# Casts of the weights rank first among ready work when the engines' queues are laid out

## The chip, the core and the metric

The kernel runs on one core of one Trainium2 chip. The metric is the device time of one execution in microseconds (us); a kernel's time is the median over its runs. The core's engines are TensorE (PE, the matrix products), VectorE (DVE), ScalarE (ACT), GpSimd (POOL) and SyncE (SP, which issues DMAs here). Each works through a queue of its own, in the order in which the program was laid out.

## What is computed

Two blocks follow one another on 512 tokens of width 1024, all in float32. The first is a half step of SwiGLU, an attention stage of two branches (a native sparse one, NSA, and a sliding window with sinks, SWA), and another half step of SwiGLU. The second is an adaptive normalisation, a mixer (HGRN2 on one half of the width, S5 on the other), and a PEER layer: 8 heads pick experts by two products of keys, and the outputs of 16384 experts of one unit each are summed.

```python
h = h + 0.5 * swiglu(rmsnorm(h), ffn1_gate, ffn1_up, ffn1_down)
u = rmsnorm(h); q, k, v, ... = split(u @ w_in)
merged = sigmoid(ga) * (nsa(...) @ w_branch_a) + sigmoid(gb) * (swa(...) @ w_branch_b)
h = h + merged @ w_out
h = h + 0.5 * swiglu(rmsnorm(h), ffn2_gate, ffn2_up, ffn2_down)
x = rmsnorm(h)
...
x = x + gt1 * (concat(hgrn2(q, f, i, g), s5(u)) @ w_out)
x = x + gt2 * peer(h2, peer_wq, keys1, keys2, peer_u, peer_v)
return rmsnorm(x)
```

## The kernel before

Every product with a weight goes the same way. `Prog.weight` loads a tile of 128x1024 float32 (`raw`) by a DMA that SP issues, ACT copies it to fp32r, the format that the matmuls take (`whi`, L173), and DVE subtracts the two for the rest (`wlo`, L174; on POOL in a part of the first PEER stage, while `pool_lo` is set). The activations are split alike (`xhi`, `xlo`). `mm3` then makes three matmuls of one: `whi` by `xhi`, `whi` by `xlo`, `wlo` by `xhi`, all into one PSUM tile `ps`. The line of all matmuls is L82, that of the transposes L86. I call the two casts the hi cast and the lo cast.

The tiles `raw`, `whi` and `wlo` come from the pool `w` with three buffers each. So the hi cast of a weight writes over that of the third weight before it, and can't start until PE has read that one for the last time. `Weights.take` prepares a weight up to two ahead of its use (`AHEAD = 2`).

The order of the work is set twice. The program is written as generators, which `weave` lets take turns by an estimated clock; that gives every instruction its rank. Then the scheduler of the tile framework lays out the queue of each engine: among the instructions that are ready by its estimate, the one of the lowest rank number is put next. The result is fixed when the kernel is built. On the chip each engine takes its queue strictly from the front, and an instruction at the front that waits for a buffer or an operand holds up all that stand behind it.

The names and lines that come up below: in attention, `t` are the scores' exponentials (ACT, L923 in NSA and L966 in SWA), `sums` their sums, `fac` the reciprocal (DVE L927 and L973), by which DVE scales `t` (L934, L976). PE transposes `t` (L86), ACT and DVE copy the transposes out of PSUM (L656), and PE multiplies them with the values (`nat`). In the mixer, `hg_head` builds a head's decay in seven levels: PE multiplies, DVE takes the level over by a predicated copy (L1326) and makes the next operands (L1308, L1309). In the second PEER stage the activations come back from memory, POOL multiplies them with the gates, and ACT and DVE split them into `pwh` (L590) and `pwl` (L591).

Of the kernel before, what the change touches and what calls it, by code (L numbers as in the profile page):

```python
# [8 lines left out]
F32 = mybir.dt.float32  # L9
# [4 lines left out]
ALU = mybir.AluOpType  # L14
# [35 lines left out]
class Prog:  # L50
# [116 lines left out]
    def weight(self, ap, n=1024):  # L167
        nc = self.nc
        raw = self.w.tile([128, 1024], F32, tag="raw", name=self.name("raw"))
        nc.sync.dma_start(raw[:, :n], ap)  # L170
        hi = self.w.tile([128, 1024], F32R, tag="whi", name=self.name("whi"))
        lo = self.w.tile([128, 1024], F32R, tag="wlo", name=self.name("wlo"))
        nc.scalar.copy(hi[:, :n], raw[:, :n])  # L173
        (nc.gpsimd if self.pool_lo else nc.vector).tensor_tensor(lo[:, :n], raw[:, :n], hi[:, :n].bitcast(F32),  # L174
                                                                 op=ALU.subtract)
        return raw, hi, lo

    def mm3(self, ps, whi, wlo, xhi, xlo, start, stop):
# [1761 lines left out]
```

## Time and profile before

| what | value |
|---|---|
| median of 3 runs | 3066.33 us (3066.26 to 3071.9) |
| the profiled execution | 3077.48 us |
| its span, first to last instruction | 3075.7 us |
| mean granted TensorE clock | 0.992 of full speed |
| PE busy | 3007.1 us, 98% |
| DVE, ACT, POOL busy | 67%, 38%, 35% |

The profile is of one execution, which took 11.15 us more than the median; the rows' times are those of that execution. A row of the timeline gives the start, the duration, the engine, the line and operation, and, where the engine was idle before it, for how long and which instruction ended that. In the page's names `ps` is a PSUM tile and buffer numbers are left out. The stages lie about so in the span: first SwiGLU to 400 us, attention to 750, second SwiGLU and the preparation of S5 to 1185, mixer to 1475, first PEER stage (routing, then products with `peer_u` and the dense gates) to 2341, second PEER stage (products with `peer_v`) to 3062.

### The profile page before, as it was taken

Reading aid. Unit: us, or ns where it says so; the run is one execution under the profiler, and the core shown is the slowest. Engines: PE = TensorE matmul, PEld = TensorE weight load, DVE = VectorE, ACT = ScalarE, POOL = GpSimd, SP = SyncE. Lnnn points to the kernel's source line nnn. Section 1 sums busy time; section 2 is a strip of 40 time slices with the busy share of each in tenths; the row PEclk is TensorE's granted clock in tenths of the full one; section 3 lists DMA queues with packets and bytes.
Section 4 is the critical chain, followed back from the end, with each engine's and each line's share of the span. In section 5 each row is a group of like instructions: output and inputs, shape, how many; then the busy total and the mean of one; then the engine's idle time right before and its main releaser. Section 6 shows DMA issues by size and latency. Waiting matters only on the chain.

```text
span 3075.7 us, 39979 instructions
## 1 busy us (share of the span) xinstructions
PE 3007.1 (98%) x14672; PEld 2473.4 (80%) x14672; DVE 2058.7 (67%) x3797; ACT 1167.1 (38%) x1851; POOL 1091.0 (35%) x1025
## 2 busy tenths in 40 slices
PE   8999999999999999899999899999999999999998
PEld 7888876667887889787888778888887888888887
DVE  7455467775768656874778999878773656655653
ACT  4222334453422235443434344444443322332232
POOL 1000110002353422012345798878772423322321
PEclk9999999999999999999999999999999999999999
DMA  6344322113535443222333355555558656555642
GB/s 203 109 143 132 102 81 83 49 39 100 164 117 184 161 127 117 77 71 83 99 110 117 127 185 188 190 179 197 186 185 268 215 192 205 192 187 190 204 137 76
DMA packets 140323, 443.53 MB, mean 144 GB/s; under 512 B 16720, under 2 KB 19568, under 8 KB 135008
## 3 DMA queue, kind: packets, MB, share of 16 engines
q1 hardware_dynamic: 82512, 285.41, 28.9%
q10 hardware_dynamic: 42624, 101.73, 9.0%
q0 software_dynamic: 14992, 53.85, 5.5%
q8 instruction: 116, 1.90, 0.3%
q14 instruction: 79, 0.65, 0.1%
HBM read 361.88 MB, written 77.86 MB: 143 GB/s over the span
## 4 chain that ended last, share of the span: by engine, by line
PE 70%; DVE 6%; issue 1%; POOL 1%; DMA 1%; ACT 1%; ACTq 0%; DVEq 0%; POOLq 0%
PE ps L82 69%; DVE wlo L174 1%; PE ps L86 1%; DMA t<-act_d 1%; DVE b L1570 1%; POOL t L823 0%; POOL eq L1550 0%; DVE eq L1546 0%; ACT whi L173 0%; DMA act_d<-t 0%; DVE sel L1553 0%; POOL t L1687 0%; DVE stage L1595 0%; DVE h L1817 0%; ACT t L966 0%
## 5 line engine op out<-in xcount | busy, mean ns | idle before, releaser
L173 ACT CAST whi<-raw 128x1024 fp32r<-128x1024 f32 (+2 forms) x505 | 516.9, 1026 | 1113.9 <-PE ps L82 881.2
L82 PE MATMUL ps<-xhi,whi 128*128 128x512 f32 (+1 forms) x2232 | 875.2, 393 | 12.2 <-ACT whi L173 9.8
L82 PE MATMUL ps<-xhi,wlo 128*128 128x512 f32 (+1 forms) x2232 | 864.2, 388 | 9.6 <-DVE wlo L174 9.5
L82 PE MATMUL ps<-xlo,whi 128*128 128x512 f32 (+1 forms) x2232 | 864.2, 388 | 0.8 <-DVE xlo L382 0.7
L174 DVE TENSOR_TENSOR wlo<-raw,whi 128x1024 fp32r<-128x1024 f32 (+2 forms) x476 | 610.9, 1284 | 129.1 <-ACT whi L173 118.9
L82 PEld LDWEIGHTS ps<-xhi,whi 128*128 128x128 f32 x2232 | 421.8, 189 | 105.6 <-issue 14.1
L82 PEld LDWEIGHTS ps<-xhi,wlo 128*128 128x128 f32 x2232 | 421.3, 189 | 99.7 <-DVE wlo L174 12.4
L82 PEld LDWEIGHTS ps<-xlo,whi 128*128 128x128 f32 x2232 | 421.6, 189 | 80.8 <-issue 2.5
L1569 POOL TENSOR_SCALAR a<-iota,routeT 128x128 fp32r<-128x128 f32 x512 | 452.5, 900 | 95.6 <-PE ps L82 91.7
L82 PE MATMUL ps<-pwh,wlo 128*128 128x512 f32 (+1 forms) x1048 | 402.5, 384 | 2.1 <-DVE wlo L174 2.1
L82 PE MATMUL ps<-pwh,whi 128*128 128x512 f32 (+1 forms) x1048 | 402.9, 385 | 1.1 <-ACT pwh L590 1.1
L82 PE MATMUL ps<-pwl,whi 128*128 128x512 f32 (+1 forms) x1048 | 402.8, 384 | 0.2 <-DVE pwl L591 0.2
L1687 POOL TENSOR_TENSOR t<-t,gt 128x512 f32<-128x512 f32 x128 | 196.6, 1556 | 422.9 <-DMA t<-act_d 389.0
L1570 DVE SCALAR_TENSOR_TENSOR b<-iota,routeT,routeG 128x256 fp32r<-128x256 f32 x512 | 242.8, 523 | 63.7 <-PE ps L82 63.7
L1823 DVE SCALAR_TENSOR_TENSOR h<-ps,mod,h 128x512 f32<-128x512 f32 (+1 forms) x131 | 96.3, 735 | 218.4 <-PE ps L82 218.4
L82 PEld LDWEIGHTS ps<-pwh,wlo 128*128 128x128 f32 x1048 | 196.9, 188 | 41.4 <-DVE wlo L174 2.6
L82 PEld LDWEIGHTS ps<-pwh,whi 128*128 128x128 f32 x1048 | 196.9, 188 | 40.6 <-ACT pwh L590 1.8
L82 PEld LDWEIGHTS ps<-pwl,whi 128*128 128x128 f32 x1048 | 196.9, 188 | 39.9 <-DVE pwl L591 1.0
L1594 ACT COPY stage<-ps 128x256 f32<-128x256 f32 x256 | 137.8, 643 | 151.2 <-PE ps L82 142.3
L591 DVE TENSOR_TENSOR pwl<-t,pwh 128x512 fp32r<-128x512 f32 x128 | 141.0, 1128 | 46.7 <-ACT pwh L590 42.1
L268 POOL TENSOR_TENSOR acc<-acc,sq 128x512 f32<-128x512 f32 x18 | 32.0, 1777 | 382.4 <-ACT sq L264 382.0
L1595 DVE TENSOR_TENSOR stage<-stage,ps 128x256 f32<-128x256 f32 x256 | 146.8, 620 | 2.3 <-ACT stage L1594 2.3
(407 smaller groups left out, 3841.5 us busy)
## 6 DMA issues: line engine op xcount, KB each, us to landing
raw<-pu SPq DMA_DIRECT2D x128, 512.0 KB, 3.6
raw<-pv SPq DMA_DIRECT2D x128, 512.0 KB, 3.5
act_d<-t ACTq DMA_DIRECT2D x128, 256.0 KB, 2.8
gates_d<-stage ACTq DMA_DIRECT2D x32, 1024.0 KB, 4.2
gt<-gates_d POOLq DMA_DIRECT2D x16, 2048.0 KB, 13.6
t<-act_d ACTq DMA_DIRECT2D x128, 256.0 KB, 3.6
aw<-ada_w SPq DMA_DIRECT2D x48, 512.0 KB, 4.5
raw<-g SPq DMA_DIRECT2D x44, 512.0 KB, 3.6
```

The lines of the kernel that those rows point to most:

```text
L82: self.nc.tensor.matmul(out, lhsT=lhsT, rhs=rhs, start=start, stop=stop)
L86: self.nc.tensor.transpose(out, x, ident)
L173: nc.scalar.copy(hi[:, :n], raw[:, :n])
L174: (nc.gpsimd if self.pool_lo else nc.vector).tensor_tensor(lo[:, :n], raw[:, :n], hi[:, :n].bitcast(F32), op=ALU.subtract)
L268: nc.gpsimd.tensor_tensor(st["acc"], st["acc"], sq, op=ALU.add)
L591: self.nc.vector.tensor_tensor(lo, x, hi.bitcast(F32), op=ALU.subtract)
L1569: g.tensor_scalar(a[:, i, :], iota, T2[0][:, c], None, op0=ALU.is_equal)
L1570: v.scalar_tensor_tensor(b[:, i], iota[:, None, :].to_broadcast([128, 2, 128]), T2[1][:, c], TG[:, t + i, :, None].to_broadcast([128, 2, 1 ...
L1594: nc.scalar.copy(sv, pv[:, :, 0])
L1595: v.tensor_tensor(sv, sv, pv[:, :, 1], op=ALU.add)
L1687: g.tensor_tensor(f(t), f(t), gts[e // 8][:, :, e % 8, :], op=ALU.mult)
L1823: nc.vector.scalar_tensor_tensor(x, ps, P.mod[:, 40 + d:41 + d], x, op0=ALU.mult, op1=ALU.add)
```

## The change

The two casts in `Prog.weight` are put under `high_priority()`. This gives them the first rank among ready work when the queues are laid out, in place of the rank of their position in the program. No instruction is added, taken away or altered, and on the chip nothing is ranked: only places in the five queues differ.

```diff
-        nc.scalar.copy(hi[:, :n], raw[:, :n])
-        (nc.gpsimd if self.pool_lo else nc.vector).tensor_tensor(lo[:, :n], raw[:, :n], hi[:, :n].bitcast(F32),
-                                                                 op=ALU.subtract)
+
+        with self.tc.high_priority():
+            nc.scalar.copy(hi[:, :n], raw[:, :n])
+            (nc.gpsimd if self.pool_lo else nc.vector).tensor_tensor(lo[:, :n], raw[:, :n], hi[:, :n].bitcast(F32),
+                                                                     op=ALU.subtract)
```

The lines behind the edit move down by two. Of some 13,790 instructions that the queue of PE holds, 193 rows of a comparison differ, of 3,511 on DVE 332, of 2,021 on ACT 177, of 1,030 on POOL 13, on SP none. The lo casts `wlo_7295`, `wlo_7853`, `wlo_14230`, `wlo_14265`, `wlo_14309`, `wlo_14344` have the same neighbours in both orders, and so have all rows of PE from 1780 to 2341 us and all rows of all engines from 2400 us on. The number behind a name is that of the tile, in the order of the program.

The first place is at 650 us, in the last NSA block. ACT computes the exponentials of four score tiles in eight instructions, and the order there was:

```order
L923 ACTIVATE t_5137,sums_5121<-ps_5123,mx_5120 128x256 x2
L923 ACTIVATE t_5149,sums_5121<-ps_5140,mx_5120 128x256 x2
L923 ACTIVATE t_5155,sums_5121<-ps_5141,mx_5120 128x256 x2
L885 ACTIVATE cm_5183,sums_5197<-cm_5183,mx_5196 128x31 x8
L656 COPY t_5228<-ps_5218 128x512
L173 CAST whi_5238<-raw_5236 128x1024
```

It is now the following, on ACT:

```order
L925 ACTIVATE t_5137,sums_5121<-ps_5123,mx_5120 128x256 x2
L925 ACTIVATE t_5149,sums_5121<-ps_5140,mx_5120 128x256 x2
L925 ACTIVATE t_5155,sums_5121<-ps_5141,mx_5120 128x256
L175 CAST whi_5238<-raw_5236 128x1024
L925 ACTIVATE t_5155,sums_5121<-ps_5141,mx_5120 128x256
L887 ACTIVATE cm_5183,sums_5197<-cm_5183,mx_5196 128x31 x8
L658 COPY t_5228<-ps_5218 128x512
```

The hi cast of weight 5238 has gone ahead of the last exponential, of eight instructions on `cm` and of a copy. On DVE, at the same place, the reciprocal of the sums was followed by the scaling, and the lo cast came later:

```order
L927 RECIPROCAL fac_5158<-sums_5121 128x8
L931 TENSOR_TENSOR fac_5158<-fac_5158,gates 128x8
L934 TENSOR_SCALAR t_5131<-t_5131,fac_5158 128x256 x2
L934 TENSOR_SCALAR t_5149<-t_5149,fac_5158 128x256 x2
L934 TENSOR_SCALAR t_5137<-t_5137,fac_5158 128x256 x2
L934 TENSOR_SCALAR t_5155<-t_5155,fac_5158 128x256 x2
L888 RECIPROCAL fac_5208<-sums_5197 128x8
L889 TENSOR_TENSOR fac_5208<-fac_5208,gates 128x8
L656 COPY t_5230<-ps_5219 128x512
L892 TENSOR_TENSOR cm_5183<-cm_5183,fac_5208 128x248
L811 TENSOR_TENSOR t_5232<-ps_5091,rb_2797 128x512
L174 TENSOR_TENSOR wlo_5239<-raw_5236,whi_5238 128x1024
```

After the change the lo cast stands ahead of the reciprocal, on DVE:

```order
L885 TENSOR_SCALAR mx_5196<-mx_5196 128x8
L176 TENSOR_TENSOR wlo_5239<-raw_5236,whi_5238 128x1024
L929 RECIPROCAL fac_5158<-sums_5121 128x8
L933 TENSOR_TENSOR fac_5158<-fac_5158,gates 128x8
L936 TENSOR_SCALAR t_5131<-t_5131,fac_5158 128x256 x2
L936 TENSOR_SCALAR t_5149<-t_5149,fac_5158 128x256 x2
```

So the reciprocal and all scaling rows are now behind a cast that waits for the hi cast.

The second place is at 608 us, in SWA, on DVE. `t_4746` and `t_4782` are transposes that PE needs for the products with the values; before:

```order
L969 TENSOR_TENSOR es_4679<-mx_4677,sinks 128x8
L656 COPY t_4746<-ps_4735 128x512
L971 TENSOR_TENSOR sums_4678<-sums_4678,es_4679 128x8
L811 TENSOR_TENSOR t_4754<-ps_4646,rb_2797 128x512
L973 RECIPROCAL fac_4723<-sums_4678 128x8
L656 COPY t_4782<-ps_4771 128x512
L976 TENSOR_SCALAR t_4690<-t_4690,fac_4723 128x256 x2
L976 TENSOR_SCALAR t_4710<-t_4710,fac_4723 128x256 x2
L976 TENSOR_SCALAR t_4697<-t_4697,fac_4723 128x256 x2
L976 TENSOR_SCALAR t_4717<-t_4717,fac_4723 128x256 x2
L656 COPY t_2734<-ps_4733 128x128
L174 TENSOR_TENSOR wlo_4832<-raw_4829,whi_4831 128x1024
```

After the change, the same stretch of DVE reads:

```order
L971 TENSOR_TENSOR es_4679<-mx_4677,sinks 128x8
L176 TENSOR_TENSOR wlo_4832<-raw_4829,whi_4831 128x1024
L973 TENSOR_TENSOR sums_4678<-sums_4678,es_4679 128x8
L658 COPY t_4746<-ps_4735 128x512
L975 RECIPROCAL fac_4723<-sums_4678 128x8
L813 TENSOR_TENSOR t_4754<-ps_4646,rb_2797 128x512
L978 TENSOR_SCALAR t_4690<-t_4690,fac_4723 128x256 x2
L978 TENSOR_SCALAR t_4710<-t_4710,fac_4723 128x256 x2
L978 TENSOR_SCALAR t_4697<-t_4697,fac_4723 128x256 x2
L978 TENSOR_SCALAR t_4717<-t_4717,fac_4723 128x256 x2
L658 COPY t_4782<-ps_4771 128x512
```

The lo cast 4832 has moved from the row behind the scaling to the row ahead of `sums_4678`, and with it the copies `t_4746` and `t_4782` have moved back. On ACT the hi cast 4831 has moved ahead of `es_4679` and of the copy of `t_4744`. Of the same kind are `wlo_4761` and the copy `t_4635` (596 us), `wlo_3712` and the copy `t_3700` (494 us), and `wlo_5423` with the scaling of `t_5374` (675 us).

The third place is at 1258 us, the last levels of an HGRN2 head, on DVE. Before:

```order
L1018 TENSOR_TENSOR t_10082<-t_9793 128x4x64 x2
L1326 COPY_PREDICATED t_9842<-c_lvl,ps_10077 128x512
L174 TENSOR_TENSOR wlo_10098<-raw_10095,whi_10097 128x1024
L1308 TENSOR_TENSOR t_10082<-t_9792,t_10082 128x4x64
L1309 TENSOR_TENSOR t_10082<-t_9801,t_10082 128x4x64
L1326 COPY_PREDICATED t_9842<-c_lvl,ps_10113 128x512
```

After the change DVE goes through the same levels so:

```order
L1020 TENSOR_TENSOR t_10082<-t_9793 128x4x64 x2
L1328 COPY_PREDICATED t_9842<-c_lvl,ps_10077 128x512
L658 COPY t_10143<-ps_9804 128x8x16
L1310 TENSOR_TENSOR t_10082<-t_9792,t_10082 128x4x64
L1311 TENSOR_TENSOR t_10082<-t_9801,t_10082 128x4x64
L1328 COPY_PREDICATED t_9842<-c_lvl,ps_10113 128x512
```

The lo cast 10098 is gone from between them, since it and the lo casts 10020 and 10167 now stand 51, 63 and 35 rows ahead of the row L1310 here, among earlier levels; `wlo_10167` stood behind all levels before. A copy of `t_10143` has moved forward too. At the begin of the second PEER stage (2390 us) the move goes the other way: `wlo_20877`, which stood ahead of `pwl_20980` and `pwl_21019`, now stands behind both.

## Rows read from the trace of the kernel before

**Rows 1.** the page, busy time of each engine

```profile
PE 3007.1 (98%) x14672; PEld 2473.4 (80%) x14672; DVE 2058.7 (67%) x3797; ACT 1167.1 (38%) x1851; POOL 1091.0 (35%) x1025
```

**Rows 2.** the page's groups: count | busy, mean ns | idle before, releaser

```profile
L173 ACT CAST whi<-raw 128x1024 fp32r<-128x1024 f32 (+2 forms) x505 | 516.9, 1026 | 1113.9 <-PE ps L82 881.2
```

**Rows 3.** waits of PE: us in total, times, longest

```profile
PE ps L82 <- DVE wlo L174: 15.6, 9, 3.4
PE ps L82 <- ACT whi L173: 11.0, 3, 9.8
```

**Rows 4.** instructions of tile wlo, 1696 to 1728 us: who waited for it

```profile
  PE ps L82: 8.4, 4
```

**Rows 5.** windows, PE alone: busy (instructions), PEclk, DMA share, GB/s

```profile
1780.00:2340.00 560.00, 559.96 (x2678) 1.00 0.56 193
1709.00:1712.00 3.00, 3.00 (x7) 0.50 0.78 236
```

**Rows 6.** timeline at 2388 to 2399 us, begin of the second PEER stage

```profile
2387.77 1.23 DVE L174 TENSOR_TENSOR wlo<-raw,whi 128x1024 fp32r<-128x1024 f32 x1 [0.83 <-ACT whi L173]
...
2388.91 4.31 DVE L591 TENSOR_TENSOR pwl<-t,pwh 128x512 fp32r<-128x512 f32 x3
...
2394.70 4.42 DVE L174 TENSOR_TENSOR wlo<-raw,whi 128x1024 fp32r<-128x1024 f32 x1 [0.82 <-ACT whi L173]
...
2399.18 0.50 PE L82 MATMUL ps<-pwh,wlo 128*128 128x512 f32 x1 [2.14 <-DVE wlo L174]
```

**Rows 7.** timeline at 650 us: start, us, engine, line, [idle before <-releaser]

```profile
650.75 0.48 ACT L923 ACTIVATE t<-ps,mx 128x256 f32<-128x256 f32 x1
...
651.35 0.20 DVE L927 RECIPROCAL fac<-sums 128x8 f32<-128x8 f32 x1 [0.86 <-ACT t L923]
...
652.28 1.35 PE L86 MATMUL ps<-ident,t 128*128 128x128 f32 x5 [1.45 <-DVE t L934]
...
654.09 1.06 ACT L173 CAST whi<-raw 128x1024 fp32r<-128x1024 f32 x1
```

**Rows 8.** timeline at 1260 us, a head of HGRN2

```profile
1260.28 0.72 DVE L1326 COPY_PREDICATED t<-c_lvl,ps 128x512 f32<-128x512 int32 x1
...
1260.50 2.04 PE L82 MATMUL ps<-t 128*128 128x128 f32 x8 [2.92 <-DVE t L1309]
...
1264.00 1.21 DVE L174 TENSOR_TENSOR wlo<-raw,whi 128x1024 fp32r<-128x1024 f32 x1
```

**Rows 9.** timeline at 607 to 610 us

```profile
607.83 0.68 DVE L656 COPY t<-ps 128x512 f32<-128x512 f32 x1
...
609.45 0.23 ACT L970 ACTIVATE es<-es 128x8 f32<-128x8 f32 x1
...
610.02 1.09 ACT L173 CAST whi<-raw 128x1024 fp32r<-128x1024 f32 x1
...
610.21 1.08 PE L82 MATMUL ps<-t,nat 128*64 128x512 f32 x4 [0.66 <-ACT t L656]
```

**Rows 10.** timeline at two more places in the attention stage

```profile
493.66 0.41 DVE L656 COPY t<-ps 128x256 f32<-128x256 f32 x1
...
495.15 0.65 PE L82 MATMUL ps<-t,nat 128*64 128x256 f32 x4 [0.49 <-ACT t L656]
...
595.97 0.68 DVE L656 COPY t<-ps 128x512 f32<-128x512 f32 x1
...
597.53 1.08 PE L82 MATMUL ps<-t,nat 128*64 128x512 f32 x4 [0.48 <-ACT t L656]
```

**Rows 11.** windows: us, busy (instructions) of PE, PEld, DVE, ACT, POOL, PEclk

```profile
911.53:922.50 10.97, 9.89 (x44) 7.86 (x42) 10.97 (x3) 1.68 (x2) 10.94 (x11) 1.00 0.07 25
1224.00:1261.00 37.00, 28.35 (x161) 27.02 (x161) 36.43 (x85) 13.72 (x21) 0.00 (x0) 0.92 0.10 31
```

**Rows 12.** timeline, two single rows of DVE and PE

```profile
911.53 10.97 DVE L174 TENSOR_TENSOR wlo<-raw,whi 128x1024 fp32r<-128x1024 f32 x1
...
1708.89 0.79 PE L82 MATMUL ps<-xhi,wlo 128*128 128x512 f32 x1 [3.43 <-DVE wlo L174]
```

## The prediction

> **What bounds the kernel now.** I read the busy times first: PE is busy 3007.1 of the span's 3075.7 us [rows 1], so what a change can win is bounded by the other 69 us, and what it loses is whatever new wait it puts on PE. Then the group of the hi casts: in front of them ACT is idle 1113.9 us, and 881.2 of these end with a matmul of PE [rows 2]. Most casts, then, wait for the buffer of the third weight before them, which PE still reads. A cast that waits for a buffer gains nothing from a better place in its queue.
>
> Then the waits of PE. Over the whole execution PE waits 15.6 us, nine times, for a lo cast, and 11.0 us, three times, for a hi cast, of which 9.8 us are one wait, the first weight at the program's start [rows 3]. So the casts that the change promotes cost PE at most 15.6 + 11.0 - 9.8 = 16.8 us. Of the 15.6 us, 8.4 lie in four waits at the end of PEER's routing, 1696 to 1728 us [rows 4]. Last I looked at the dense stage, 1780 to 2340 us: PE is busy 559.96 of 560.00 us [rows 5], no wait is left there to take away.
>
> **What the change takes away.** The four casts behind the 8.4 us (14230, 14265, 14309, 14344) and the one with the slow row below (7295) keep their neighbours in the new order. They were already at the place where the scheduler thought their buffer free; on the chip DVE is simply full there. What the promotion can reach is less than the other 16.8 - 8.4 = 8.4 us, and one wait of that, 2.14 us at 2399 us [rows 6], belongs to a stage where a neighbouring cast moves back. I take 0 for the gain, with up to 2 us as the better end: the waits for hi casts other than the first sum to 1.2 us [rows 3], and in the NSA compression, where those casts do move forward, PE then finds the lo cast late in their place.
>
> **What it adds, place by place.** Every term is a cast that now stands ahead of a row that PE waits for. The durations are 1.06 us for the hi cast [rows 7] and 1.21 for the lo cast [rows 8].
>
> At 650 us PE waits 1.45 us for the scaled exponentials already [rows 7]. The last exponential starts at 650.75 us. In the new order the hi cast 5238 runs first, 650.75 to 651.81, and the last exponential with its sum ends near 652.4 instead of 651.3. DVE has the lo cast at its front, starts it when the hi cast is done, at about 651.85, and ends near 653.06. Only then comes the reciprocal, which ran at 651.35: 1.7 us late, and the transposes of PE behind it as much. PE's rows ahead of them are unchanged, so nothing covers it: +1.7, wait 3.2 in all.
>
> At 608 us PE waits 0.66 us for ACT's copy of a transpose [rows 9]. ACT would start the hi cast 4831 at 609.45 in place of 610.02, so that the copy is about 1.1 late. The other copy that PE's row at 610.21 needs, `t_4746`, ran at 607.83 [rows 9]; it now stands behind the lo cast (about 610.55 to 611.75) and the sums, and ends near 612.5, 2.3 us after PE wants it. PE gets some of that back, since one of the four products is moved behind its next weight and a later wait for the same kind of copy closes. Between 1.1 and 2.3 I take +1.6.
>
> Three more places in attention have this pattern. At 596 us the copy `t_4635` moves from 595.97 to behind the lo cast, and PE wants it at 597.53 [rows 10]; it would end near 599.85, but PE's next rows waited for the scaling anyway, which ends only about 0.9 later: +0.9. At 494 us the copy `t_3700` moves from 493.66 to behind both casts, near 496.8, and PE's product of 495.15 [rows 10] needs it; about 0.65 us of other matmuls move ahead to cover it: +1.0. At 675 us the scaling of `t_5374` goes behind both casts, 1.5 us late, with some 0.4 us of slack: +1.1. Together +3.0, the ends being 0.9 (matmuls pulled forward cover the rest) and 2.3 + 1.6 + 1.5 = 5.4 (nothing is covered).
>
> In the HGRN2 head PE waits 2.92 us until 1260.50 for DVE [rows 8], which is full from 1224 to 1261 us, with 36.43 of 37.00 us busy [rows 11]. Three lo casts move further ahead on DVE, which changes nothing for the last level as long as they were ahead of it. The fourth, 10167, ran at 1264.00, behind the levels [rows 8], and now runs ahead of them, with one small copy: 1.21 + 0.14 = +1.4 in front of the last level. The ends are 0 (a matmul group pulled forward on PE covers it) and 2.4 (DVE also waits for the hi cast's buffer once more).
>
> At the begin of the second PEER stage the lo cast 20877 moves from 2387.77 to behind two of the three `pwl` rows that ran from 2388.91 to 2393.22 [rows 6] and a row of `h`. It would end near 2394.4. PE wanted the lo cast after it at 2399.18 - 2.14 = 2397.0 [rows 6], and goes through the 24 matmuls of a weight in 24 x 560/2678 = 5.0 us [rows 5], so it wants 20877 near 2392.0: a new wait of 2.4 us. The wait of 2.14 us, for a cast that took 4.42 us [rows 6], is then swallowed, at least in part. Between -2.1 and +2.4 I take +0.5.
>
> The rest (one or two rows moved at 630 us, at the begin of the mixer, and at its end) is below 0.3 us a place: +0.3 in all, 0 to 1.5. In the dense stage some thirty hi casts go ahead of one gelu and its DMA, and lo casts ahead of one or two additions; PE's order is the same and PE has no wait there [rows 5], so 0.
>
> A longer wait costs once more when the clock falls. After the wait of 3.43 us that ended at 1708.89 [rows 12] PE ran 3.0 us at a granted clock of 0.50, that is at 1.2 GHz [rows 5]: half of them, 1.5 us, are lost. The wait at 650 us would grow to this length. I take +1.0, between 0 and 3.
>
> **A rule on this.** The lo cast at 911.53 us took 10.97 us [rows 12], nine times a usual one, while POOL was busy through the stretch [rows 11]. The Trainium skill, page "SBUF — State Buffer", section "SBUF: two separate sides", says that VectorE and GpSimd share a pair of ports under an exclusive lock, and that the loser is blocked until the other's instruction is done. By that rule one POOL instruction is the most that a cast waits, and a cast moved next to POOL's work would cost some 10.94/11 = 1.0 us [rows 11]; by the row it is up to 10.97 - 1.21 = 9.8, over most of the eleven instructions that POOL ran there. The sum is the same by either, since no cast of the terms above stands beside POOL's runs except 20877.
>
> **The sum.** 1.7 + 1.6 + 3.0 + 1.4 + 0.5 + 0.3 + 1.0 = +9.5 us. The profiled execution would come to 3077.5 + 9.5 = 3087.0, and the median, which lies 11.2 below it, to 3075.8. The lower ends sum to 1.7 + 1.1 + 0.9 + 0 - 2.1 + 0 + 0 - 2 = -0.4 (3066), the upper to 1.7 + 2.3 + 5.4 + 2.4 + 2.4 + 1.5 + 3.0 = 18.7 (3085).
>
> **Rivals.** First, nothing measurable. 881.2 us of waiting for buffers [rows 2] say that the rank of a cast seldom matters, and the scheduler that promoted the casts also reordered PE's queue around them, to put matmuls where it saw a gap. If these cover the attention places, what stays is the 650 us place and the HGRN2 head, 1.7 + 1.4 = 3.1 us: 3069.4. Against it: at 650 us and at 608 us the rows of PE ahead of the wait are the same ones. 0.30.
>
> Second, faster. Queues laid out otherwise meet POOL otherwise. The slow lo casts of 10.97 and of 4.42 us are meetings of DVE and POOL; if the shifts upstream dissolve such meetings, PE gets back up to what it waits for lo casts outside routing, 15.6 - 8.4 = 7.2 us [rows 3, 4], and 3059.1 follows if the terms above come to nothing. It decides only where attention and HGRN2 cost less than the few us that dissolve, and nothing in the order moves these casts: 0.07.
>
> Third, much slower. In the dense stage each promoted hi cast waits at ACT's front for PE to free its buffer and holds the gelu behind it, which holds a PSUM tile. If the eight PSUM tiles don't cover a delay of 1.06 us, thirty places cost up to 1 us each on top: +9.5 + 30 = 3106 at the worst, 3085 to 3090 more likely. It decides once PE's busy share there drops below 0.98; it is 0.9999 now [rows 5], and DVE and ACT have room. 0.08. The page's rule would give a smaller version, a moved cast slowed by one POOL instruction, within the range.
>
> **How the numbers follow.** The likeliest is the sum, 0.55: 3075.8, its own range 3071 to 3083. About 0.2% (6.1 us) is what a measurement of this kernel can tell from no change. Slower than that are most of the forecast's range and the third rival: 0.57. Within it are the first rival and the lower edge of the forecast: 0.36. Faster: 0.07. Taking 0.1 off either side gives 3065 to 3083.
>
> **What would show it.** In the new profile: at 650 us a wait of PE for L936 (L934 before) of some 3 us in place of 1.45; a wait for a L658 copy of about 2 us near 610; the four waits at 1696 to 1728 us still there, 8 us or so; PE still without a gap from 1780 to 2340; the waits of PE for lo casts in total no smaller than 12 us. I would be wrong if PE's waits in attention grow by less than 3 us, which says that the moved matmuls cover the moved casts, or if the 8.4 us at the end of routing vanish, which says that casts wait there for rank after all.

## The result, and the profile after the change

The changed kernel takes 3096.85 us (median of 4 runs, 3093.16 to 3100.8) beside 3068.32 us for the kernel before on the same chip (4 runs, 3066.26 to 3071.9). The ratio is 1.0078, 95% interval [1.0063, 1.0093], so the change costs some 24 us (19 to 28.5, the interval times 3068). The forecast was slower, by 9.5 us, within 3065 to 3083 us: the direction came true, the size did not, and 3096.85 lies above the range.

The two profiled executions stand closer than the medians: spans of 3093.3 and 3075.7 us, 17.6 apart, because the profiled execution of before, 3077.48 us, was longer than each of its four timed runs. Places are compared between traces below, and sizes between timed runs.

The page of the changed kernel, the busy times and the hi and lo casts, to be read against [rows 1, 2]:

```profile
PE 3016.1 (98%) x14672; PEld 2476.9 (80%) x14672; DVE 2073.8 (67%) x3797; ACT 1167.4 (38%) x1851; POOL 1086.4 (35%) x1025
...
L175 ACT CAST whi<-raw 128x1024 fp32r<-128x1024 f32 (+2 forms) x505 | 517.1, 1026 | 1168.8 <-PE ps L82 952.2
L176 DVE TENSOR_TENSOR wlo<-raw,whi 128x1024 fp32r<-128x1024 f32 (+2 forms) x476 | 619.5, 1302 | 139.3 <-ACT whi L175 128.9
```

The casts wait longer than before: ACT stands idle in front of hi casts for PE 952.2 us, where it was 881.2. No cast got faster by its rank; it only stands at the front of its queue sooner, with other rows behind it. The waits of PE (us in total, times, longest), to be read against [rows 3]:

```profile
PE ps L82 <- DVE wlo L176: 16.9, 10, 3.7
PE ps L82 <- ACT whi L175: 9.2, 1, 9.2
PE ps L82 <- ACT t L658: 7.6, 6, 2.3
```

The waits for lo casts went from 15.6 to 16.9 us, and those for ACT's copies of transposes from 2.3 us in five waits to 7.6 in six. Where the loss lies is best read in stretches with the same number of matmuls. Windows of PE, first before, then after (us, busy and matmuls, granted clock, DMA share, GB/s):

```profile
440.00:700.00 260.00, 248.76 (x1363) 0.99 0.19 60
```

```profile
440.00:713.00 273.00, 256.14 (x1363) 0.98 0.19 58
```

As many matmuls of the attention stage, 1363, take 13 us more: 5.6 us of it is idle time (16.9 in place of 11.2 us), the rest is time in which PE counts as busy. What that is, is taken apart in the section on the prediction. In the dense stage nothing changed; after, to be read against [rows 5]:

```profile
1800.00:2370.00 570.00, 570.00 (x2729) 1.00 0.57 196
```

Rows that stand in both traces, by when each starts, give the delay as it builds up. The difference grows from -0.47 us at the last cast ahead of the NSA compression (439.27 before, 438.80 after) to +12.46 at the end of attention (700.48, 712.94), is +12.11 in the mixer (1394.98, 1407.09), +13.78 when PEER begins (1495.46, 1509.24), +15.53 at PE's wait in the routing ([rows 12] 1708.89, here 1724.42), and +17.66 in the second PEER stage (2437.14, 2454.80).

Each of these is one execution against one. How far they scatter can be read from the traces of the experiments below, where a stretch has the order of before while the rank is given elsewhere. The stretches between the rows named above, in us:

| Stretch, ending with | Before | Changed | Traces with the order of before there |
|---|---|---|---|
| the end of attention | 261.21 | 274.14 | 260.09 to 261.67 (5) |
| the row in the mixer | 694.50 | 694.15 | 689.65 to 694.57 (4) |
| the begin of PEER | 100.48 | 102.15 | 98.92 to 100.50 (3) |
| PE's wait in the routing | 213.43 | 215.18 | 213.42 to 213.44 (4) |
| the row in the second PEER stage | 728.25 | 730.38 | 725.58 to 732.13 (3) |

So the losses in attention, ahead of PEER and in the routing are clear of chance. The differences in the mixer and in the second PEER stage are not, and in the mixer the trace of before is itself a long one: three of the four others lie between 689.65 and 690.95.

### The profile page after: what moved, and what is told of

Read it like the earlier page. It is cut to its first block, busy times and chain, and to the rows that moved or that the text cites. A ratio compares the mean times of both kernels' runs of the same rounds, so it can differ in the third digit from the quotient of the medians.

```text
span 3093.3 us, 40019 instructions
## 1 busy us (share of the span) xinstructions
PE 3016.1 (98%) x14672; PEld 2476.9 (80%) x14672; DVE 2073.8 (67%) x3797; ACT 1167.4 (38%) x1851; POOL 1086.4 (35%) x1025
## 4 chain that ended last, share of the span: by engine, by line
PE 69%; DVE 7%; issue 1%; DMA 1%; ACT 1%; POOL 1%; DVEq 0%; ACTq 0%; POOLq 0%
PE ps L82 69%; DVE wlo L176 2%; PE ps L86 1%; POOL t L825 0%; DMA t<-act_d 0%; DMA aw<-ada_w 0%; DVE eq L1548 0%; DVE b L1572 0%; POOL eq L1552 0%; ACT whi L175 0%; DVE sel L1555 0%; DMA act_d<-t 0%; ACT t L968 0%; DVE h L1819 0%; ACT t L925 0%
## 5 line engine op out<-in xcount | busy, mean ns | idle before, releaser
L175 ACT CAST whi<-raw 128x1024 fp32r<-128x1024 f32 (+2 forms) x505 | 517.1, 1026 | 1168.8 <-PE ps L82 952.2
L176 DVE TENSOR_TENSOR wlo<-raw,whi 128x1024 fp32r<-128x1024 f32 (+2 forms) x476 | 619.5, 1302 | 139.3 <-ACT whi L175 128.9
```

## The experiments

Where the rank is given in one part of the program only, the order of each engine's queue is that of the changed kernel in that part and that of before elsewhere. Differences in us are the ratio of the timed runs and its interval times the median of before on the same chip.

**1. Which stage costs.** The edit, with the switch set ahead of a stage:

```diff
-        nc.scalar.copy(hi[:, :n], raw[:, :n])
-        (nc.gpsimd if self.pool_lo else nc.vector).tensor_tensor(lo[:, :n], raw[:, :n], hi[:, :n].bitcast(F32),
-                                                                 op=ALU.subtract)
+        with self.tc.high_priority() if self.rank0 else nullcontext():
+            nc.scalar.copy(hi[:, :n], raw[:, :n])
+        with self.tc.high_priority() if self.rank0 else nullcontext():
+            (nc.gpsimd if self.pool_lo else nc.vector).tensor_tensor(lo[:, :n], raw[:, :n], hi[:, :n].bitcast(F32),
+                                                                     op=ALU.subtract)
...
+        P.rank0 = True
         P.open("att", 1376)
...
+        P.rank0 = False
         P.open("ffn2", 640)
```

Attention alone:

> The casts rank first in the attention stage alone (400 to 750 us); every other stage has the order of before. If the loss sits at the attention places, as the trace after has it (12.9 us more between 450 and 700 us), this is 11 to 15 us slower than before. If the sum of the prediction was right about attention (6.3 us there) and the rest of the loss lies elsewhere, 5 to 8.

The mixer alone, and PEER alone (the switch on ahead of each):

> The casts rank first in the mixer alone. The prediction had +1.5 us here, the trace after shows PE 5.6 us late in the HGRN2 head at 1257 us and back to +0.3 by 1390. If a wait there is given back, 0 to +2; if it stays, +4 to +6.

> The casts rank first in the two PEER stages alone. The prediction had +0.5 us. The trace after has PE 5.5 us later at the end than it was at 1485 us. If that is the order's doing, +4 to +6; if these waits come and go from run to run (POOL and DVE meeting), -2 to +2.

All but attention (on from the start, off in attention):

> The casts rank first everywhere but in attention. The complement of the first run: together they should make the 24 us of the change. By the traces +3 to +6 us; if the loss is spread over the later stages, +12 to +18.

Measured, beside 3072.77 us for before (27 runs): attention alone 3086.65, 1.0040 [1.0028, 1.0052], +12.3 us (8.6 to 16.0); the mixer alone 3074.27, 1.0005 [0.9997, 1.0014], +1.5; PEER alone 3078.07, 1.0017 [1.0007, 1.0028], +5.2 (2.2 to 8.6); all but attention 3082.11, 1.0027 [1.0018, 1.0037], +8.3 (5.5 to 11.4). Attention and all but attention sum to 20.6, inside the change's 19 to 28.5, so the parts add up. Attention carries the largest part, 12.3 of the 20.6.

**2. Which cast costs.** `rank0` stays on for the whole program, but for one of the two casts:

```diff
+        with self.tc.high_priority() if self.rank0 else nullcontext():
+            nc.scalar.copy(hi[:, :n], raw[:, :n])
+        with self.tc.high_priority() if False else nullcontext():
+            (nc.gpsimd if self.pool_lo else nc.vector).tensor_tensor(lo[:, :n], raw[:, :n], hi[:, :n].bitcast(F32),
+                                                                     op=ALU.subtract)
```

> Only the hi casts get the first rank; the lo casts keep the rank of before. In this order the five attention places at 494, 596, 608, 650 and 675 us stand almost as after the change, since a lo cast becomes ready, and is queued, once its hi cast is placed; the NSA compression (448 to 490 us) and the HGRN2 head stand as before. Theory of places (the cost is a cast's own time ahead of a row that PE waits for, and it is set by the hi cast): the steps after 490 us repeat, +8 to +9.5 us in attention, no step of 3 us at 485 us, and 0 to 2 at the second PEER stage: in all +8 to +12 us over before. Theory of the lo casts (a lo cast at the front of DVE's queue that waits for its hi cast is what costs, and a hi cast's rank on ACT costs nothing): +0 to +3 us.

> Only the lo casts get the first rank. In this order the compression (448 to 490 us) and the HGRN2 head stand as after the change, the attention places at 596 to 675 us nearly as before. Theory of places: +3.3 us by 490 us, +0 to 1.5 in the rest of attention, the new wait of some 5.6 us in the HGRN2 head and given back, and what belongs to PEER's routing: in all +4 to +9 us over before, so that this run and the one with the hi casts alone add up to the change. Theory of the lo casts: nearly the whole change, +15 to +24 us. In the compression DVE should stand idle some 3 us longer in front of lo casts that wait for their hi cast, with the scaling of probabilities queued behind them.

Measured, beside 3073.43 (19 runs): the hi casts alone 3082.32, 1.0031 [1.0017, 1.0044], +9.5 us; the lo casts alone 3083.31, 1.0035 [1.0022, 1.0049], +10.8 us. Both casts cost, and both sums fit the theory of places better than that of the lo casts; but the lo casts came out above their bound of 9, and their interval (6.8 to 15.1) touches the 15 of the other theory. What tells more is where each loses, in the table below.

**3. The compression by itself.** The first rank for eleven weights only (`self.nw` counts the casts of the stage):

```diff
+        with self.tc.high_priority() if 12 <= self.nw - 1 < 23 else nullcontext():
+            nc.scalar.copy(hi[:, :n], raw[:, :n])
```

> Both casts get the first rank for eleven weights alone: the last eight of the NSA compression's stage and the three behind them (440 to 490 us). The order there is that of the changed kernel, everywhere else that of before. The prediction counted this place as 0. Theory of the lo cast at the front (three lo casts move ahead of the scaling of the probabilities, DVE stands idle in front of them until their hi casts have a buffer and are done, and the scaling, the transposes and the copies come late): +3 to +5 us, with DVE's waits for hi casts between 440 and 500 us at 12 us or so in place of 6.7. Theory that the step of 3.3 us in the trace is chance, or is made good in the rest of attention: -1 to +1.5 us.

Measured 3074.4 beside 3073.21 (28 runs), 1.0006 [0.9995, 1.0018], +1.8 us (-1.5 to 5.5). The timed runs don't decide between the two theories; the trace does, for one execution. The table gives the start of four rows that stand in every trace (the lo cast of 128x688, the copy of `hid` for the values, PE's wait of 1.7 us for the scaling, the last three splits of attention), and how much longer than before each of the three stretches between them is. The second stretch holds the places at 494, 596 and 608 us, the third those at 650 and 675.

| Kernel | Starts of the four rows | Compression | 494 to 608 | 650, 675 | Sum |
|---|---|---|---|---|---|
| Before | 439.27, 485.71, 627.46, 700.48 | | | | |
| Changed | 438.80, 488.57, 636.07, 712.94 | +3.33 | +5.75 | +3.85 | +12.93 |
| Attention alone | 439.99, 489.38, 638.51, 715.02 | +2.95 | +7.38 | +3.49 | +13.82 |
| Hi casts alone | 439.78, 485.34, 631.91, 708.48 | -0.88 | +4.82 | +3.55 | +7.49 |
| Lo casts alone | 439.22, 490.89, 634.25, 706.67 | +5.23 | +1.61 | -0.60 | +6.24 |
| Compression alone | 439.45, 488.66, 630.41, 703.51 | +2.77 | 0.00 | +0.08 | +2.85 |

With the compression alone the other stretches come out as before to 0.1 us, and its own is 2.77 longer. Before and five traces with the order of before in attention (the mixer alone, PEER alone, all but attention, the second PEER stage alone, routing and dense stage alone) have 46.44 to 46.91 us for the compression and 141.73 to 141.79 for the second stretch, so the step is real and isn't made good. The lo casts make it, the hi casts don't; their +5.23 holds more of a fallen clock (0.90 over the stretch, 0.97 in the changed kernel, 1.00 before). At 494 to 608 us it is the other way round, because there a lo cast is queued where its hi cast has been placed: of the hi casts' +4.82, as of the +7.38 with attention alone, 1.7 is a fall of the clock (0.58 over 613.34 to 617.34 us; 0.78 and 0.80 in the last section), which leaves 3.1 beside the lo casts' 1.61 at a clock of 1.00. The third stretch says less: with the order of before it is 72.98 to 73.10 us in five traces, but 71.48 in that of the second PEER stage alone, where a fall of the clock that the others have at 654 us doesn't come. It doesn't come with the lo casts alone either (1.00 over their stretch), so that their -0.60 is no gain.

At the compression the reciprocal and the scaling of the four rows ran in one go before, behind lo casts that DVE did not have to wait for:

```profile
465.11 0.17 DVE L927 RECIPROCAL fac<-sums 128x4 f32<-128x4 f32 x1
...
465.70 1.67 DVE L934 TENSOR_SCALAR t<-t,fac 128x512 f32<-128x512 f32 x4
```

Rows of the changed kernel's timeline at the same place (start, us, engine, line, [idle before <-releaser]):

```profile
465.42 1.05 ACT L175 CAST whi<-raw 128x1024 fp32r<-128x1024 f32 x1 [0.98 <-DMA raw<-cw1v]
466.50 1.23 DVE L176 TENSOR_TENSOR wlo<-raw,whi 128x1024 fp32r<-128x1024 f32 x1 [1.42 <-ACT whi L175]
...
467.64 0.17 DVE L929 RECIPROCAL fac<-sums 128x4 f32<-128x4 f32 x1
...
468.23 0.49 DVE L936 TENSOR_SCALAR t<-t,fac 128x512 f32<-128x512 f32 x1
468.64 1.22 DVE L176 TENSOR_TENSOR wlo<-raw,whi 128x1024 fp32r<-128x1024 f32 x1
...
469.77 1.27 DVE L936 TENSOR_SCALAR t<-t,fac 128x512 f32<-128x512 f32 x3
...
473.76 0.65 PE L82 MATMUL ps<-t,nat 128*64 128x256 f32 x2 [1.56 <-ACT t L658]
```

The hi cast waits for its weight to be loaded, DVE stands idle 1.42 us in front of the lo cast that needs it, and the reciprocal and the scaling run only after it; a second lo cast goes between the first scaling row and the other three. The copies and matmuls that use the scaled rows are late, and PE waits 1.56 us. DVE's idle time in front of lo casts over attention, from the view of waits, first before (440 to 700 us), then after (440 to 713), then the hi casts alone (440 to 707):

```profile
DVE wlo L174 <- ACT whi L173: 14.8, 12, 3.2
```

```profile
DVE wlo L176 <- ACT whi L175: 26.2, 16, 3.3
```

```profile
DVE wlo L177 <- ACT whi L175: 22.8, 16, 3.2
```

With the lo casts alone it is 16.6 us in 13 waits. The total is not the price: 2.55 us of the change's growth lie at 450 us, where DVE before stood idle 3.21 us for PE instead. What sorts the kernels is DVE's idle time at the place of the scaling: from 455 to 490 us it is 0.3 us before and with the hi casts alone, 2.4 after the change, 2.2 with the lo casts alone and 1.7 with the compression alone, and the last three are those that lose here.

**4. PEER by halves.** The switch on ahead of the second stage only, and off ahead of it:

```diff
+        self.rank0 = True
         self.open("peer2", 1216)
```

> Both casts get the first rank in the second PEER stage (from about 2350 us) alone. PEER as a whole measured +5.2 us [2.1 to 8.6] where 0.5 was forecast. If the second stage's begin carries it: +3 to +6 us, with a new wait of PE for a pwh or pwl row near 2382 us that isn't made good at 2410. If it lies in the routing (1700 to 1790 us) or in the dense stage: -1 to +2.5 us.

> First rank in PEER's routing and dense stage alone (1485 to 2350 us). PEER as a whole measured +5.2 us [2.1 to 8.6], its second stage +4.0 [0.3 to 7.4]. If the second stage carries it all, and the thirty hi casts ahead of a gelu in the dense stage are free: 0 to +2 us, with PE busy 0.9999 of the dense stage. If the hi casts hold up the gelus, or casts in the routing hold up what PE waits for: +3 to +6 us.

Measured: the second stage alone 3077.9 beside 3073.43, 1.0013 [1.0001, 1.0024], +4.0 us (0.3 to 7.4); routing and dense stage alone 3076.06 beside 3073.21, 1.0012 [1.0, 1.0025], +3.7 us (0 to 7.7). Both intervals reach from next to nothing to more than the whole, so the timed runs don't split it. With the dense stage at a busy share of 1 (570.00 of 570.00 us in the changed kernel), the first half's share must come ahead of it. In the trace of the routing and dense stage alone a wait appears that before doesn't have, two waits ahead of the 3.43 us of [rows 12]:

```profile
1698.12 0.50 PE L83 MATMUL ps<-xhi,wlo 128*128 128x512 f32 x1 [0.87 <-DVE wlo L177]
```

The next one, 0.87 us before (until 1699.73), is 1.11 us here. Over the routing the waits for lo casts are 9.5 us in five, in the changed kernel 10.9 in five, where [rows 4] has 8.4 in four:

```profile
  PE ps L82: 10.9, 5
```

**5. Lo casts off DVE.** No rank; in attention POOL does the lo casts:

```diff
+        P.pool_lo = True
         P.open("att", 1376)
```

> No cast gets a rank; in the attention stage alone the lo casts run on POOL in place of DVE, where they take some 2.4 us in place of 1.2. If lo casts standing among DVE's rows are a cost of attention already before the change, PE's waits for DVE and ACT rows there shrink: -2 to -8 us. If POOL's slower casts, or DVE and POOL side by side, cost more than that: +1 to +10 us, with new waits of PE for lo casts at 440 to 700 us.

Measured 3094.42 beside 3073.43, 1.0067 [1.0051, 1.0084], +20.6 us. Worse than either theory said. PE's waits between 440 and 720 us:

```profile
PE ps L87 <- DVE t L937: 6.1, 4, 2.1
PE ps L83 <- ACT t L659: 4.7, 5, 2.9
...
PE ps L83 <- POOL wlo L177: 2.1, 1, 2.1
```

PE waits for POOL's lo cast once; most of the new waits are for DVE's scaling and ACT's copies, as after the change. Rows of the trace show why the scaling is late with the casts gone from DVE. Four scaling rows beside POOL's lo casts take 5.87 us; four others, between two runs of POOL's casts, take 1.68, as such rows did before (1.67):

```profile
461.98 5.87 DVE L937 TENSOR_SCALAR t<-t,fac 128x512 f32<-128x512 f32 x4
462.71 7.37 POOL L177 TENSOR_TENSOR wlo<-raw,whi 128x1024 fp32r<-128x1024 f32 x3 [6.26 <-ACT whi L175]
...
470.23 1.68 DVE L937 TENSOR_SCALAR t<-t,fac 128x512 f32<-128x512 f32 x4
```

So this run does not test what lo casts on DVE cost before the change: it adds a cost of its own.

**6. The opposite rank.** Both casts 150 rows later than written, in attention, and in the whole program:

```diff
+        with self.tc.high_priority(offset=-150) if self.late else nullcontext():
+            nc.scalar.copy(hi[:, :n], raw[:, :n])
```

> The opposite rank, in the attention stage alone: both casts get a rank 150 rows later than written. Only casts between 448 and 490 us and those at 494, 640 and 675 us move back by one to three rows of DVE. If rows of attention behind casts cost time already before the change: -1 to -4 us. If PE then waits for the lo casts that come later, in place of the rows that come sooner: +1 to +4 us. A reading within 1 us either way says that the order of before is at its best here, as far as casts go.

> The opposite rank in the whole program, 150 rows later than written. If a cast's rank matters on both sides of the order of before (the theory of places): lo casts come late in PEER's routing, where DVE is full, and +3 to +15 us follow, with PE's waits for lo casts well above 15.6 us in all. If casts nearly always wait for a buffer and rank is of no weight: -2 to +2 us.

Measured beside 3073.21: in attention 3074.6, 1.0005 [0.9995, 1.0015], +1.5 us (-1.5 to 4.6), which decides nothing; everywhere 3094.94, 1.0067 [1.0049, 1.0086], +20.6 us. Of the 20.6, 11 are the first weight, for which PE waits at the program's start:

```profile
20.85 0.79 PE L82 MATMUL ps<-xhi,whi 128*128 128x512 f32 x1 [20.85 <-ACT whi L174]
```

In the kernel before that wait is 9.8 us [rows 3]. Of the other 9.6 us, the waits for lo casts, 19.0 us in all, have 3.4, and those for hi casts behind the first, 3.7 us, have 2.4; the rest was not assigned. So the price of rank has two sides: casts too early hold what PE wants, casts too late are what PE wants.

**7. The waited-for rows first.** No rank for casts; attention's sums with the sinks, reciprocals, scaling and copies of transposes get a rank 300 rows earlier:

```diff
+                with self.tc.high_priority(offset=300):
+                    self.evac(s[:n, :128 * nh], pt[:n, :128 * nh])
...
+            with self.tc.high_priority(offset=300):
+                nc.vector.tensor_tensor(es, mx, sinks, op=ALU.add)
...
```

> No cast gets a rank. In attention the rows that PE waits for (the sums with the sinks, the reciprocals, the scaling of the probabilities, the copies of transposes) get a rank 300 rows earlier than written. If the casts of the order before already stand ahead of such rows at a cost, as they do by more after the change: -2 to -6 us, with PE's waits for copies of transposes and for scaled probabilities below the 2.3 and 1.4 us of before. If DVE's and ACT's rows there stand where their inputs arrive, so that an earlier rank finds nothing to move: -1.5 to +2 us.

Measured 3069.72 (11 runs) beside 3073.72 (15 runs), 0.9987 [0.9978, 0.9996], -4.0 us (-6.8 to -1.2): faster than both kernels, by little. The four rows start at 440.55, 487.69, 627.71 and 698.99, so the stretches are +0.70, -1.73 and -1.74 us beside before. PE's waits between 440 and 700 us have the copies at 0.8 us, before 2.3, and the scaling at 1.0, before 1.4:

```profile
PE ps L86 <- DVE t L936: 1.0, 1, 1.0
PE ps L82 <- ACT t L656: 0.8, 2, 0.5
```

The -1.73 of the second stretch is the order's doing, since it scatters by 0.06 with the order of before. The -1.74 of the third is not, but for 0.20: the fall of the clock at 654 us doesn't come (1.00), as in the trace of the second PEER stage alone, where this stretch takes 71.48 us and here 71.28.

## Why the prediction was wrong in size

**Right: the direction, its reason, and the gain of nothing.** Casts wait for buffers, so rank wins them nothing: PE's waits for lo casts were to stay at 12 us or more and are 16.9; the routing's waits were to stay and did, 10.9 us; the dense stage was to keep PE without a gap, and the third rival, hi casts that hold up gelus and with them PSUM tiles, fell with 570.00 of 570.00. The place at 650 us was forecast with a wait of some 3 us, and it is 2.96:

```profile
660.98 1.04 ACT L175 CAST whi<-raw 128x1024 fp32r<-128x1024 f32 x1
...
662.06 1.23 DVE L176 TENSOR_TENSOR wlo<-raw,whi 128x1024 fp32r<-128x1024 f32 x1 [1.30 <-ACT whi L175]
...
663.20 0.20 DVE L929 RECIPROCAL fac<-sums 128x8 f32<-128x8 f32 x1
...
664.13 1.17 PE L86 MATMUL ps<-ident,t 128*128 128x128 f32 x4 [2.96 <-DVE t L936]
```

**Wrong: "in the NSA compression PE then finds the lo cast late in their place", taken as 0.** It measured +3.33 us in the trace of the change and +2.77 by itself. About 1.7 of the 3.33 is a fall of the clock (below). I had looked at the hi casts that move forward and at PE's waits for casts, and not at what the three lo casts that move with them stand in front of: the scaling of the probabilities.

**Too small: the places at 494, 596 and 608 us,** 1.0 + 0.9 + 1.6 = 3.5, where the stretch is 5.75 longer, at a granted clock of 1.00 in both traces. By rows of PE that stand in both (499.12 and 503.23, 602.92 and 608.90, 615.94 and 624.55) the delay grows by 1.25 at the first place, 1.87 at the second and 2.63 at the third. How late the casts make the copies was right. After, at the 608 us place:

```profile
615.41 1.04 ACT L175 CAST whi<-raw 128x1024 fp32r<-128x1024 f32 x1 [0.50 <-ACT t L968]
...
616.49 1.22 DVE L176 TENSOR_TENSOR wlo<-raw,whi 128x1024 fp32r<-128x1024 f32 x1 [3.25 <-ACT whi L175]
...
617.63 0.16 DVE L973 TENSOR_TENSOR sums<-sums,es 128x8 f32<-128x8 f32 x1
617.71 0.68 DVE L658 COPY t<-ps 128x512 f32<-128x512 f32 x1
```

The hi cast stands behind exponentials and starts at 615.41, and DVE does nothing for 3.25 us. The copy behind the lo cast had run 1.62 us ahead of the exponential of `es` before [rows 9, 607.83 and 609.45]; now it runs 1.35 us behind it (616.36, 617.71). At 596 us the same idle time is 2.12 us (the lo cast of 602.44). The sum had this: `t_4746` was to end 3.3 us after PE starts the last matmul ahead of the products (609.16 before, 612.5), and it ends 3.2 us after it (615.17, 618.39). That DVE doesn't go on to a ready row is what these rows show. The Trainium skill, page "TensorE: Matmul & The Clock Gate", section "Architectural detail: the array is 16× 32×32, not 1× 128×128", says that the queues of ACT and DVE are strict FIFO, and this trace agrees with its 3.25 us.

What was mis-sized is what the late copies cost PE. The prediction took something off for products that move behind the next weight; but four products with the values that ran in one row of 1.08 us [rows 9, 10] now run in two pairs, and a pair alone takes 1.07. At 596 us:

```profile
603.50 1.07 PE L82 MATMUL ps<-t,nat 128*64 128x512 f32 x2 [2.31 <-ACT t L658]
...
605.12 1.07 PE L82 MATMUL ps<-t,nat 128*64 128x512 f32 x2
```

Over the windows of attention the busy time of such products grows, while their number and the mean of one stay the same, first before, then after:

```profile
L82 PE MATMUL ps<-t,nat 128*64 128x512 f32 x52 | 14.1, 614 | 1.5 <-ACT t L656 1.5
```

```profile
L82 PE MATMUL ps<-t,nat 128*64 128x512 f32 x52 | 16.3, 614 | 4.1 <-ACT t L658 3.8 <-DVE t L658 0.3
```

Those of 128x256 go from 18.9 to 20.2 us in the same way, so that 3.5 us of attention's 13 are products in rows that were broken up.

**Too small: the clock, +1.0.** Windows of PE in which the granted clock fell for a part of the time to 0.5, that is from 2.4 to 1.2 GHz, first before, then after:

```profile
654.00:658.00 4.00, 4.00 (x13) 0.57 0.00 0
```

```profile
476.00:479.00 3.00, 3.00 (x17) 0.53 0.60 194
479.00:482.00 3.00, 3.00 (x22) 0.90 0.00 0
636.00:640.00 4.00, 3.93 (x15) 0.58 0.00 0
664.00:668.00 4.00, 3.87 (x14) 0.58 0.40 131
```

At 0.57 of the full clock 4 us lose 4 x 0.43 = 1.7 us. After, 1.4 + 0.3 + 1.7 + 1.7 = 5.1 are lost, 3.4 more. The term stood for the wait at 650 us, which grows; but that one had its fall already before (654 us, here 664). The new ones stand behind waits of 1.56 and 0.68 us at 473 to 476 us, and behind one of 1.70 us at 636. Both falls lie outside the second stretch, which ends at 636.07. Without them the compression has lost 3.33 - 1.7 = 1.6 us, the places at 494 to 608 us all of their 5.75, and the last two 3.85 - 1.7 = 2.1, where 0, 3.5 and 1.7 + 1.1 = 2.8 were forecast. The 13 us of attention are then 5.6 of idle time, 3.4 of clock and 3.5 of products in pairs; 0.5 stays open. Whether a fall comes at a given wait differs between traces with the same order (last section), so the 3.4 belong to these two traces.

**Open: the HGRN2 head, +1.4.** A wait of 5.57 us came, but others shrank: PE's waits there sum to 9.1 us (1238 to 1279 us), before to 8.6 (1225 to 1266). The delay's fall from +12.46 to +12.11 says nothing, since that stretch scatters by 4.9 us with the order of before. Alone the mixer's moves measured +1.5 (-0.9 to 4.3), which the term fits.

**Too small: PEER, 0.5 + 0.3.** Alone it measured +5.2. Two pieces are clear in the traces: +1.67 by the begin of PEER (13.78 - 12.11), where PE now waits 0.57 and 0.70 us for two rows `xlo` of the norm, and +1.75 by the routing, where a wait of 0.87 us is new (until 1708.42) and the next grows from 0.87 to 1.09. The first stretch takes 102.10 to 102.15 us in all five traces with the lo casts ranked there and 98.92 to 100.56 with the order of before or the hi casts alone; the second takes 215.17 to 215.21 us in all five with the hi casts ranked and 213.42 to 213.44 with the order of before or the lo casts alone. I had put the first among "one or two rows moved" and took 0 for the routing, since its four slow casts keep their neighbours. They do; a fifth, of 3.42 us in both traces (1689.40, 1704.95), now comes too late for PE. The second stage's share stays open: +2.13 from the routing to it (17.66 - 15.53) lies within the scatter of 725.58 to 732.13 us, and 4.0 us timed has an interval from 0.3.

**Uncertain: the step from the trace to the median, "which lies 11.2 below it".** The sum gave 3087.0 for a profiled execution, and that one measured 3095.04, 8.0 more. The other 13.0 of the 21 us between 3075.8 and 3096.85 come from where two single executions lie among the runs of their kernels: that of before 11.2 above its median, that of the changed kernel 1.8 below its own. This does not excuse the terms. The timed runs need no such step and give 24 us (19 to 28.5), and the parts timed alone 12.3 + 1.5 + 5.2 = 19.0, for terms of 9.5; the trace of before, long in the mixer, hides a part of that. By the parts, attention was 12.3 where 6.3 of places and 1.0 of clock were forecast, PEER 5.2 where 0.8 was.

The first rival (nothing measurable, because PE's reordered queue covers the casts) fell with attention's 12.3 us, and the second (faster, as meetings of DVE and POOL dissolve) with the ratio.

## What to carry to other kernels

Before a producer is ranked ahead of other ready work, ask what stands behind it in an in-order queue and when its own input is really there. Its price is not its duration alone: the engine stands idle at it until its input comes, and that costs where rows that the bound engine wants stand behind it. Then ask what the bound engine does with operands that come late and in pieces; here four products of one row came in pairs, and each pair took as long as the four. Rank the rows that the bound engine waits for, not those that wait for the bound engine; here the first won 4 us where the second lost 24. And take the spread of a kernel's own runs before a profiled time is turned into a median.

## What was not expected of the hardware

Waits of the same length, at the same place in the program, don't always bring the clock down. Before, PE waits 1.73 us until 627.46 and then runs at full clock; after, the same row waits 1.70 us until 636.07, and the clock is 0.58 (the window 636 to 640 us above). The other way round at 596 us: after a wait of 2.31 us until 603.50 the change runs at 1.00, while with the rank in attention alone PE waits 2.29 us there, until 604.28, and the clock falls. First before, then the change, then attention alone:

```profile
627.00:632.00 5.00, 4.54 (x28) 1.00 0.00 0
```

```profile
604.00:608.00 4.00, 4.00 (x20) 1.00 0.40 131
```

```profile
604.00:608.00 4.00, 3.72 (x8) 0.78 0.44 131
608.00:612.00 4.00, 4.00 (x25) 0.80 0.01 4
```

At 650 us PE waits 1.45 us before the change and the clock falls (654 to 658 us above); in the trace of the second PEER stage alone, with the same order there, PE waits 1.46 us until 654.57, and it doesn't:

```profile
656.00:660.00 4.00, 4.00 (x25) 1.00 0.00 0
```

Which wait costs twice could not be read from its length.

And the begin of the second PEER stage scatters with its order unchanged: PE's waits there, over the same rows, sum to 3.5 us before (2362 to 2415 us), 3.8 with the rank in attention alone, 1.6 with the rank in the mixer alone and 1.3 with that in the compression alone. The wait for a lo cast among them is 2.1, 2.5, 0.2 and none. A term of 1 us at such a place can't be read from one trace.
